# A decoder step on one core: x and the vectors taken from the host as features by tokens, the first gate and up run together, the first norm's sums spread out, and X's tiles moved in SBUF

## The chip, the cores and the metric

The kernel runs on one NeuronCore of one Trainium2 chip, as one program. The metric is the device time of one execution in microseconds (us). Engines are named as in the profile: PE is the matrix engine (PEld its weight loads), DVE the vector engine, ACT the scalar engine, POOL GpSimd, SP the engine that only issues DMAs here. A row "x5" counts instructions; DMAs are issued on the queue of the engine that is named.

## The reference

One inference step of a hybrid decoder layer, all in float32: 16 learned meta tokens and 256 prompt tokens, and 8 sequences of 4 sample tokens, together 304 tokens of width 2048.

```python
x = x + 0.5 * swiglu(rmsnorm(x, norm_ffn1), ffn1_w_gate, ffn1_w_up, ffn1_w_down)   # inner width 5632
z = rmsnorm(x, norm_mix) @ w_in                        # 6144 columns: u_pool, u_ssm, gates a and b
gates = sigmoid(z[..., 2048:] + b_gate)
a_out = pool_mix(u_pool, ...)                          # causal mean pooling, then 4 group matrices
s_out = gelu(s5_scan(u_ssm, ...)); s_out = s_out * sigmoid(s_out @ glu_w + glu_b)
merged = gate_a * (a_out @ w_branch_a) + gate_b * (s_out @ w_branch_b)
x = x + merged @ w_out
x = x + 0.5 * swiglu(rmsnorm(x, norm_ffn2), ffn2_w_gate, ffn2_w_up, ffn2_w_down)
y = rmsnorm(x, final_norm)
```

Here `swiglu(x, g, u, d) = (silu(x @ g) * (x @ u)) @ d`. Outputs are y for prompt and sample tokens and the new states of pooling and scan.

## The kernel before, in words

**Layout.** Activations lie with features on the 128 partitions and tokens along the free axis, 304 columns in the first feed-forward part and 288 (without meta tokens) later. A matmul has 128x128 of a weight as the stationary operand and 304 or 288 tokens moving.

**Precision.** Each float32 weight and activation is split into a high and a low part of a narrower format, and every product is three matmuls (`mm3`, L238 to L240): high times high, high weight times low activation, low weight times high activation. X holds the split norm input (without the factor 1/rms, which is applied to the result), H the split inner activations, Y the mixer's.

**Weights.** They are read once, in chunks of 4 x 128 rows by 256 columns (512 KB), in the order of one list. `Weights.load` issues a chunk's DMA on the SP queue (L132) into one of 3 buffers `raw`, `high` has ACT cast it to `whi` (L139), `low` has DVE take `wlo` = raw - whi (L148), `take` hands both to PE. `whi` and `wlo` have 4 buffers each. One chunk feeds 24 matmuls.

**Order.** Nothing is scheduled by a tool: each engine runs its instructions in the order in which the Python code emits them. After each chunk's matmuls `step` emits the next `high`, then what was posted (the work on a finished projection), the next `low`, the next `load`, and a few instructions of side work (the tables and scan of the S5 part, on DVE, ACT and POOL, paced by a rate per chunk).

**Stages.** ffn1 goes through 22 pairs of 128 inner columns: gate with 4 chunks, up with 4 chunks, 48 x 2 x 2 = 192 matmuls a pair; `gated` multiplies gate by 1/rms and applies silu, `upped` does up and the product, and `down` follows every second pair. Then come w_in, the pooling branch, the gates. In the mixer, `gated` stores its results z to DRAM on the SP queue, 8 times two tiles `msc` (L1079) for branch a, and 8 times two tiles `gsc` (L1087) for the gates of branch b, between the weight loads of that queue. The scan is side work on DVE at that time. Then come glu, branch b, w_out, ffn2, and the last norm.

**The opening.** x comes from the host as tokens by features. `load_x` fetches quarters of 512 features on SP (five DMAs each), turns them with PE's transposes (`tx`, L410), copies them to `x`, makes X, and has ACT square the tokens with a running sum (`sqt`, L417). `load_vectors` fetches the eight norm, bias and scale vectors on POOL and turns them on PE too (`vt`, L195). These are emitted between the chunks of pair 0's gate. The factor 1/rms is put on the diagonal of a matrix, and PE spreads it over the partitions (`rb`, L357); DVE copies it to `rs_y` (L362) and `gated` uses it (L455).

**PSUM.** Eight banks: four for projections (`pj`), three for smaller work, one long-lived.

Of the kernel before, what the change touches and what calls it, by code (L numbers as in the profile page):

```python
# [45 lines left out]
POOLRATE = 3.5  # L46
LATE = 8
LAG = 2
ROWS = 15
MAGIC = 12582912.0  # L50
RSQRT_BITS = 1597463007.0 - 2147483648.0
VROWS = {"norm_ffn1": (0, 16), "norm_mix": (16, 16), "norm_ffn2": (32, 16), "final_norm": (48, 16),
         "b_gate": (64, 32), "pool_scale": (96, 8), "ssm_d": (104, 8), "glu_b": (112, 8)}


# [24 lines left out]
def weight_order():  # L80

    def cols(name, c0, kd):
        return [(name, k0, KC, c0) for k0 in range(0, kd, KC)]

    def ffn_order(i):
        out = []
        down = lambda c: [(f"ffn{i}_w_down", c * FC, FC, q * 256) for q in range(8)]
        for p in range(NF // 2):
            out += cols(f"ffn{i}_w_gate", p * 256, KD) + cols(f"ffn{i}_w_up", p * 256, KD)
            if p >= 3 and p % 2 == 1:  # L90
                out += down((p - 3) // 2)
# [12 lines left out]
    for p in range(KW // 2):  # L104
        out += cols("glu_w", p * 256, KW)
    for p in range(KD // 2):
        out += cols("w_branch_b", p * 256, KW)
    for p in range(KD // 2):
        out += cols("w_out", p * 256, KD)
    return out + ffn_order(2)  # L110


class Weights:
# [8 lines left out]
    def load(self):  # L122
# [10 lines left out]
        self.loaded += 1  # L133

    def high(self):
        i = self.nhi
# [22 lines left out]
def setup(ctx, tc, I):  # L159
# [18 lines left out]
    nc.vector.memset(g.ones, 1.0)  # L178
    g.vec = g.const.tile([P, 120], F32, name="vec")
    g.hc = g.const.tile([P, NT + NTV + 2], F32, name="hc")  # L180
    return g


def load_vectors(g, pool):

    nc, I = g.nc, g.I
    vr = pool.tile([P, P], F32, name="vr")
    for name, (r0, n) in VROWS.items():
        src = I[name] if name == "final_norm" else I[name][0]
        nc.gpsimd.dma_start(vr[r0:r0 + n], src.rearrange("(k p) -> k p", p=P))  # L190
    nc.gpsimd.dma_start(g.hc, I["consts"])

    def turn(r0, n):
        ps = bank(g, "vt", aux=True)
        nc.tensor.transpose(ps[:, :n], vr[:n], g.ident[:n, :n])  # L195
        nc.vector.tensor_copy(g.vec[:, r0:n], ps[:, r0:n])

    return turn

# [42 lines left out]

def warm(g, func):

    t = g.act.tile([P, 1], F32, tag="warm", name=nm(g, "warm"))
    g.nc.scalar.activation(t, g.ones[:, :1], func)

# [33 lines left out]
class Norm:  # L281

    def __init__(self, g, gain, n, which):
        self.g, self.gain, self.n, self.which = g, gain, n, which
        self.x = []
        self.acc = None
        self.sqs = []
        self.ss = self.r = None  # L290
        self.toks = [(0, P), (P, P), (n - P, P)]
# [38 lines left out]
    def inverse(self):  # L330

        g, nc = self.g, self.g.nc
        y = g.act.tile([P, 3], F32, tag="rt", name=nm(g, "rt"))
        if self.ss is None:
            self.summed()
            ps = bank(g, "ss", aux=True)
            for i, (t0, tn) in enumerate(self.toks):
                nc.tensor.matmul(ps[:, 2 * i:2 * i + 2], self.acc[:, t0:t0 + tn], g.ones[:, :2], start=True, stop=True)
            rsqrt(g, y, ps[:, 0:6:2], [P, 3])
        else:  # L340
            nc.vector.tensor_reduce(y, self.ss, mybir.AxisListType.X, ALU.add)
            rsqrt(g, y, y, [P, 3])
        return y
# [8 lines left out]
    def spread(self):  # L352

        g = self.g
        pr = bank(g, "rb", aux=True)
        for i, (t0, tn) in enumerate(self.toks):
# [23 lines left out]

def load_x(g, tp, norm):

    nc, I = g.nc, g.I
    xp = I["x_prompt"][0]
    xs = I["x_sample"].rearrange("b s d -> (b s) d")
    Q = KC * P
    NQ = D // Q
    tks = []
    norm.ss = tp.tile([P, 3, NQ], F32, name="ss")
    nc.vector.memset(norm.ss, 1.0)  # L390
    rest = NT - 2 * P
    norm.toks = [(0, P), (P, P), (2 * P, rest)]

    def fetch(c):
        cs = slice(c * Q, (c + 1) * Q)
        tk = [tp.tile([P, Q], F32, tag=f"tok{i}", name=nm(g, "tok"), bufs=2) for i in range(3)]
        nc.sync.dma_start(tk[0][NMETA:], xp[0:P - NMETA, cs])
        nc.sync.dma_start(tk[0][:NMETA], I["meta_tokens"][:, cs])
        nc.sync.dma_start(tk[1], xp[P - NMETA:2 * P - NMETA, cs])
        nc.sync.dma_start(tk[2][:NMETA], xp[2 * P - NMETA:, cs])  # L400
        nc.sync.dma_start(tk[2][NMETA:rest], xs[:, cs])
        tks.append(tk)

    def turn(c):
        tk = tks[c]
        pss = []
        for f in range(KC):
            ps = bank(g, "tx", aux=f % 4 != 3)
            for t, (t0, tn) in zip(tk, norm.toks):
                nc.tensor.transpose(ps[:, t0:t0 + tn], t[:tn, f * P:(f + 1) * P], g.ident[:tn, :tn])  # L410
            pss.append(ps[:, :NT])
            norm.add([pss[f]], False)
            nc.vector.tensor_copy(g.x[c * KC + f], pss[f])
        for i, t in enumerate(tk):
            tn = P if i < 2 else rest
            sq = tp.tile([P, Q], F32, tag="sqt", name=nm(g, "sqt"), bufs=1)
            nc.scalar.activation(sq[:tn], t[:tn], AF.Square, accum_out=norm.ss[:tn, i, c:c + 1])  # L417

    return fetch, turn


def proj(g, name, c0, xs, n, kd, before=None):

    ps = [bank(g, "pj")[:, :n] for _ in range(2)]
    for k0 in range(0, kd, KC):
# [11 lines left out]

def ffn(g, pool, norm, i, hpart, done, before=None, last=False):

    nc, n = g.nc, norm.n  # L440
    h = []
    nchunk = NF // FC

    def gate_up(p):
        gs = []
        pg = proj(g, f"ffn{i}_w_gate", p * 256, norm.x, n, KD, before if p == 0 else None)
        if p == 0:
            g.post.append(norm.begin)

# [8 lines left out]

        g.post.append(gated if p else lambda: g.post.append(gated))
        pu = proj(g, f"ffn{i}_w_up", p * 256, norm.x, n, KD)  # L460

        def upped():
# [5 lines left out]
            h.extend(splits(g, us, n, hpart))  # L468

        g.post.append(upped)  # L470
        if p == 0 and before is not None:
            g.started()

# [726 lines left out]
def body(ctx, tc, I, O):  # L1200
    ctx.enter_context(tc.manual_schedule())
    g = setup(ctx, tc, I)
    nc = g.nc
    n1 = Norm(g, "norm_ffn1", NT, "X")
    n2 = Norm(g, "norm_mix", NT, "X")
    xsc = [g.dram.tile([P, NL], F32, name=f"xsc{m}") for m in range(KD)]
    with ExitStack() as c1:
# [3 lines left out]
        g.x = [xpool.tile([P, NT], F32, tag="x", name=f"x{m}", bufs=KD) for m in range(KD)]  # L1211
        ct = ExitStack()
        tp = ct.enter_context(tc.tile_pool(name="tok", bufs=1))
        warm(g, AF.Silu)
        fetch, turn = load_x(g, tp, n1)
        fetch(0)
# [9 lines left out]
        def before(c):  # L1226
            if c == 0:
# [7 lines left out]
            elif c + 1 < 4:  # L1235
                turn(c + 1)
            if c == 2:
                g.w.load()
            if c == 3:
                g.w.high()  # L1240
                g.w.low()
                g.w.load()
                vturn(16, 120)

        def started():
            ct.close()
            g.side, g.rate = ssm_setup(g), SETRATE
# [8 lines left out]
        g.started = started  # L1256
        ffn(g, fpool, n1, 1, "H", done, before)
        flush(g)
# [7 lines left out]
    with ExitStack() as c2:  # L1266
# [21 lines left out]

INS = ["x_prompt", "x_sample", "state_pool", "state_ssm_re", "state_ssm_im", "meta_tokens",
       "norm_ffn1", "ffn1_w_gate", "ffn1_w_up", "ffn1_w_down", "norm_mix", "w_in", "b_gate", "pool_w",  # L1290
       "pool_scale", "ssm_lambda_re", "ssm_lambda_im", "ssm_log_dt", "ssm_b_re", "ssm_b_im", "ssm_c_re",
       "ssm_c_im", "ssm_d", "glu_w", "glu_b", "w_branch_a", "w_branch_b", "w_out", "norm_ffn2",
       "ffn2_w_gate", "ffn2_w_up", "ffn2_w_down", "final_norm"]
OUTS = [(1, NPR, D), (NB, NS, D), (1, 1, HIST, WP), (1, NB, HIST, WP),
# [18 lines left out]
```

## Time and profile before

| what | value |
|---|---|
| time, median of 3 runs | 2366.49 us (2365.99 to 2367.37) |
| profiled execution | 2366.84 us, its span 2365.0 us |
| mean granted clock of PE | 0.998 |
| PE busy | 2344.9 us, 99% of the span, 17345 instructions |
| DVE busy | 1578.7 us, 67% |
| ACT busy | 980.1 us, 41% |
| POOL busy | 85.1 us, 4% |
| moved by DMA | 426.81 MB, 180 GB/s in the mean |

The profile is of one execution. Busy times of matmuls overlap, as they are pipelined, so how fast PE goes is read from the starts of successive matmuls. A row of the timeline gives start, duration, engine, line, operation, output and inputs with sizes, count, and in square brackets the idle time ahead of it with what ended it. A row of the waits reads: engine, line and output, what ended the wait, then total us, times, longest. In the groups stand busy time in us and mean ns of one, then the idle time before.

### The profile page before, as it was taken

Reading aid. Unit: us, or ns where it says so; the run is one execution under the profiler, and the core shown is the slowest. Engines: PE = TensorE matmul, PEld = TensorE weight load, DVE = VectorE, ACT = ScalarE, POOL = GpSimd, SP = SyncE. Lnnn points to the kernel's source line nnn. Section 1 sums busy time; section 2 is a strip of 40 time slices with the busy share of each in tenths; the row PEclk is TensorE's granted clock in tenths of the full one; section 3 lists DMA queues with packets and bytes.
Section 4 is the critical chain, followed back from the end, with each engine's and each line's share of the span. In section 5 each row is a group of like instructions: output and inputs, shape, how many; then the busy total and the mean of one; then the engine's idle time right before and its main releaser. Section 6 shows DMA issues by size and latency. Waiting matters only on the chain.

```text
span 2365.0 us, 42243 instructions
## 1 busy us (share of the span) xinstructions
PE 2344.9 (99%) x17345; PEld 2316.0 (98%) x17345; DVE 1578.7 (67%) x2405; ACT 980.1 (41%) x1443; POOL 85.1 (4%) x159
## 2 busy tenths in 40 slices
PE   8999999999999999999999999999999999999997
PEld 8999999999999999999999999999999999999997
DVE  6788777777545557689999775655555555555555
ACT  5333433333543335445454544433333333333334
POOL 1000000001000002000000040000000000000000
PEclk9999999999999999999999999999999999999999
DMA  6556566657555556657676585555555555555553
GB/s 190 160 155 189 188 205 208 203 189 190 182 175 161 153 159 195 202 167 221 230 226 205 187 265 182 159 170 168 163 169 164 167 166 165 169 163 167 166 164 112
DMA packets 386033, 426.81 MB, mean 180 GB/s; under 512 B 14604, under 2 KB 376304, under 8 KB 385832
## 3 DMA queue, kind: packets, MB, share of 16 engines
q1 hardware_dynamic: 375360, 375.57, 50.9%
q0 software_dynamic: 10480, 48.54, 6.4%
q8 instruction: 136, 2.23, 0.4%
q14 instruction: 57, 0.47, 0.1%
HBM read 396.04 MB, written 28.37 MB: 179 GB/s over the span
## 4 chain that ended last, share of the span: by engine, by line
PE 98%; DVE 1%; ACT 0%; DMA 0%; SPq 0%; issue 0%; ACTq 0%; DVEq 0%
PE pj L238 24%; PE pj L239 24%; PE pj L240 24%; PE dn L238 8%; PE dn L240 8%; PE dn L239 8%; PE bu L812 1%; PE yps L828 0%; PE tx L410 0%; PE bt L758 0%; DMA tok<-in_x_sample 0%; DVE wlo L148 0%; DVE acc L327 0%; ACT y L1183 0%; PE ty L1145 0%
## 5 line engine op out<-in xcount | busy, mean ns | idle before, releaser
L148 DVE TENSOR_TENSOR wlo<-raw,whi 128x1024 fp32r<-128x1024 f32 x698 | 853.1, 1224 | 598.8 <-ACT whi L139 597.7
L139 ACT CAST whi<-raw 128x1024 fp32r<-128x1024 f32 x698 | 732.8, 1051 | 1156.7 <-PE pj L239 684.8
L238 PE MATMUL pj<-X,whi 128*128 128x304 f32 (+1 forms) x2432 | 738.4, 304 | 0.1
L239 PE MATMUL pj<-X,whi 128*128 128x304 f32 (+1 forms) x2432 | 731.6, 301 | 0.0
L240 PE MATMUL pj<-X,wlo 128*128 128x304 f32 (+1 forms) x2432 | 730.6, 300 | 0.0
L238 PE MATMUL pj<-Y,whi 128*128 128x288 f32 x1728 | 509.8, 295 | 1.6 <-DVE Y L267 1.6
L239 PE MATMUL pj<-Y,whi 128*128 128x288 f32 x1728 | 510.2, 295 | 0.0
L240 PE MATMUL pj<-Y,wlo 128*128 128x288 f32 x1728 | 509.4, 295 | 0.0
L238 PEld LDWEIGHTS pj<-X,whi 128*128 128x128 f32 x2432 | 457.7, 188 | 11.1 <-issue 10.1
L239 PEld LDWEIGHTS pj<-X,whi 128*128 128x128 f32 x2432 | 459.2, 189 | 0.0
L240 PEld LDWEIGHTS pj<-X,wlo 128*128 128x128 f32 x2432 | 459.0, 189 | 0.0
L238 PEld LDWEIGHTS pj<-Y,whi 128*128 128x128 f32 x1728 | 325.2, 188 | 4.0 <-issue 2.1
L239 PEld LDWEIGHTS pj<-Y,whi 128*128 128x128 f32 x1728 | 325.0, 188 | 0.0
L240 PEld LDWEIGHTS pj<-Y,wlo 128*128 128x128 f32 x1728 | 324.6, 188 | 0.0
L238 PE MATMUL dn<-H,whi 128*128 128x304 f32 x704 | 213.3, 303 | 0.0
L240 PE MATMUL dn<-H,wlo 128*128 128x304 f32 x704 | 213.0, 303 | 0.0
L239 PE MATMUL dn<-H,whi 128*128 128x304 f32 x704 | 212.2, 301 | 0.0
L238 PE MATMUL dn<-X,whi 128*128 128x288 f32 x704 | 208.2, 296 | 0.0
L239 PE MATMUL dn<-X,whi 128*128 128x288 f32 x704 | 207.7, 295 | 0.0
L240 PE MATMUL dn<-X,wlo 128*128 128x288 f32 x704 | 207.5, 295 | 0.0
L238 PEld LDWEIGHTS dn<-X,whi 128*128 128x128 f32 x704 | 132.6, 188 | 0.0
L239 PEld LDWEIGHTS dn<-X,whi 128*128 128x128 f32 x704 | 132.4, 188 | 0.0
(261 smaller groups left out, 1835.5 us busy)
## 6 DMA issues: line engine op xcount, KB each, us to landing
raw<-in_ffn_w_gate SPq DMA_DIRECT2D x176, 512.0 KB, 3.6
raw<-in_ffn_w_up SPq DMA_DIRECT2D x176, 512.0 KB, 3.6
raw<-in_ffn_w_down SPq DMA_DIRECT2D x176, 512.0 KB, 3.5
raw<-in_w_in SPq DMA_DIRECT2D x96, 512.0 KB, 4.1
raw<-in_w_out SPq DMA_DIRECT2D x32, 512.0 KB, 4.4
esc<-ee POOLq DMA_DIRECT2D x16, 912.0 KB, 5.0
ee<-esc POOLq DMA_DIRECT2D x16, 912.0 KB, 7.1
raw<-in_w_branch_a SPq DMA_DIRECT2D x16, 512.0 KB, 4.4
```

Source lines behind the costliest of these rows:

```text
L139: self.g.nc.scalar.copy(hi, self.raw[i])
L148: self.g.nc.vector.tensor_tensor(lo, raw, hi.bitcast(F32), ALU.subtract)
L238: mm(ps, wh, x[0], start=start, stop=False)
L239: mm(ps, wh, x[1], start=False, stop=False)
L240: mm(ps, wl, x[0], start=False, stop=stop)
L812: g.nc.tensor.matmul(ps, self.mats[i][rows, 0, ri], self.u[i][rows], start=True, stop=True)
```

## The change

The host now gives x as 16 tiles of 128 features by 304 tokens (`xt`) and all vectors as one table of 128 x 120 (`vec`). `load_x` and `load_vectors` with their transposes and copies are gone, and so are the squares by tokens. A new function `opening` fetches the first four tiles of x on ACT's queue and the rest on SP's, lets PE multiply ones nine times (`stir`), splits the first chunks of gate and up quarter by quarter as their pieces come in, and runs gate and up of pair 0 chunk by chunk in turn, into four banks. The squares of x are made tile by tile, in the opening and in pair 1's gate, and summed by DVE; the sum over features on PE and the spreading of 1/rms then stand in pair 1, whose gate uses the banks for smaller work. What follows from pair 0's results (`held`) waits for that. The side work of ffn1 starts after pair 1's gate in place of pair 0's up. The tile `warm` of the first table load moves from the pool that holds X to that of constants and grows to 64 bytes; by the allocation X's tiles start at byte 66688 of a partition in place of 66656, and follow each other by 1216 bytes as before. H's and Y's tiles start at multiples of 64 bytes before and after.

```diff
-            out += cols(f"ffn{i}_w_gate", p * 256, KD) + cols(f"ffn{i}_w_up", p * 256, KD)
+            gate, up = cols(f"ffn{i}_w_gate", p * 256, KD), cols(f"ffn{i}_w_up", p * 256, KD)
+            out += [c for pair in zip(gate, up) for c in pair] if i == 1 and p == 0 else gate + up
...
+    def parted(self, i, k):
...
+        hi, lo = self.parts[i]
+        nc.scalar.copy(hi[:, k], self.raw[i][:, k])
+        nc.vector.tensor_tensor(lo[:, k], self.raw[i][:, k], hi[:, k].bitcast(F32), ALU.subtract)
...
+    nc.scalar.dma_start(g.vec, I["vec"])
...
-    t = g.act.tile([P, 1], F32, tag="warm", name=nm(g, "warm"))
-    g.nc.scalar.activation(t, g.ones[:, :1], func)
+    t = (pool or g.act).tile([P, 16 if pool else 1], F32, tag="warm", name=nm(g, "warm"))
+    g.nc.scalar.activation(t[:, :1], g.ones[:, :1], func)
...
+def opening(g, norm):
...
+    fetch(g.nc.scalar, 0, KC)
+    warm(g, AF.Silu, g.const)
+    for k in range(KC):
+        for i in range(2):
+            g.w.piece(i, k)
+    fetch(g.nc.sync, KC, 2 * KC)
+    g.w.load()
+    stir(g)
+    for k in range(KC):
+        norm.add(x[k:k + 1], False)
+        for i in range(2):
+            g.w.parted(i, k)
...
+    for c in range(KD // KC):
...
+        for u in range(2):
...
+            step(g)
+            if u == 0 and c + 2 < KD // KC:
+                fetch(g.nc.sync, (c + 2) * KC, (c + 3) * KC)
+            if c == 3:
+                if u == 0:
+                    g.w.high()
+                    g.w.low()
+                    g.w.load()
+                squares(1 + 2 * u)
+            elif c:
+                squares(1 + u)
...
+        if p == 1 and opened is not None:
+            def before(c):
+                if c < 2:
+                    opened[1](3)
+                if c == 1:
+                    g.post.append(norm.begin)
+
+            pg = gate(before, True)
+            held[0]()
+            g.post += [held[1], gated]
+            g.started()
...
-        g.w.load()
-        fetch(1)
-        vturn = load_vectors(g, tp)
-        vturn(0, 16)
-        turn(0)
-        g.w.high()
-        g.w.low()
-        g.w.load()
...
-                fetch(2)
-                g.w.load()
-                fetch(3)
-                g.w.load()
-                turn(1)
-                g.w.high()
-                g.w.low()
...
+        opened = opening(g, n1)
```

How the instructions stand now, at three places. Numbers behind names are those of the program's tiles. First the end of the transposes and the first matmuls on PE, before:

```order
L410 MATMUL tx_259<-ident,tok_141 128x128
L410 MATMUL tx_259<-ident,tok_142 128x128
L410 MATMUL tx_259<-ident,tok_143 128x48
L238 MATMUL pj_210<-X_166,whi_204 128x304
L239 MATMUL pj_210<-X_167,whi_204 128x304
L240 MATMUL pj_210<-X_166,wlo_206 128x304
```

and PE's first rows after:

```order
L392 MATMUL stir_148<-ones 128x128 x9
L249 MATMUL pj_194<-X_158,whi_162 128x304
L250 MATMUL pj_194<-X_159,whi_162 128x304
L251 MATMUL pj_194<-X_158,wlo_163 128x304
L249 MATMUL pj_195<-X_158,whi_162 128x304
L250 MATMUL pj_195<-X_159,whi_162 128x304
L251 MATMUL pj_195<-X_158,wlo_163 128x304
L249 MATMUL pj_196<-X_158,whi_166 128x304
```

The transposes are gone, and gate (pj_194, pj_195) and up (from pj_196 on) take turns. On ACT, the first rows before:

```order
L246 ACT_TABLE_LOAD
L246 ACTIVATE warm_127<-ones 128x1
L299 ACTIVATE X_166<-tx_162,vec 128x304
L299 ACTIVATE X_175<-tx_171,vec 128x304
L299 ACTIVATE X_184<-tx_180,vec 128x304
L299 ACTIVATE X_193<-tx_189,vec 128x304
```

and after:

```order
L206 DMA vec<-in_vec 128x120
L401 DMA x_110<-in_xt 128x304
L401 DMA x_111<-in_xt 128x304
L401 DMA x_112<-in_xt 128x304
L401 DMA x_113<-in_xt 128x304
L257 ACT_TABLE_LOAD
L257 ACTIVATE warm_130<-ones 128x1
L310 ACTIVATE X_158<-x_110,vec 128x304
L156 CAST whi_162<-raw_132 128x256
L156 CAST whi_166<-raw_134 128x256
L310 ACTIVATE X_170<-x_111,vec 128x304
```

Five DMAs now stand ahead of the table load, and the casts of the first chunks come in quarters behind each X. Second, the spreading of 1/rms on PE, which stood after the first chunk of pair 0's up, before:

```order
L240 MATMUL pj_494<-X_263,wlo_456 128x304
L357 MATMUL rb_572<-dg_539,ones 128x128 x2
L357 MATMUL rb_572<-dg_539,ones 128x48
L238 MATMUL pj_493<-X_312,whi_487 128x304
L239 MATMUL pj_493<-X_313,whi_487 128x304
```

and after:

```order
L251 MATMUL pj_529<-X_432,wlo_564 128x304
L364 MATMUL rb_693<-dg_626,ones 128x128 x3
L249 MATMUL pj_704<-X_158,whi_602 128x304
L250 MATMUL pj_704<-X_159,whi_602 128x304
L251 MATMUL pj_704<-X_158,wlo_628 128x304
```

It now stands between pair 1's gate (pj_529) and its up (pj_704). Third, the SP queue in the mixer, at the first of the 16 pairs of stores of z, before:

```order
L132 DMA raw_11652<-in_w_in 128x4x256
L132 DMA raw_11705<-in_w_in 128x4x256
L132 DMA raw_11748<-in_w_branch_a 128x4x256
L132 DMA raw_11785<-in_w_branch_a 128x4x256
L1079 DMA msc_10206<-z_11612 128x288
L1079 DMA msc_10207<-z_11615 128x288
L132 DMA raw_11832<-in_w_in 128x4x256
L132 DMA raw_11865<-in_w_in 128x4x256
```

and after:

```order
L135 DMA raw_11682<-in_w_in 128x4x256
L135 DMA raw_11719<-in_w_in 128x4x256
L1133 DMA msc_10140<-z_11546 128x288
L1133 DMA msc_10141<-z_11549 128x288
L135 DMA raw_11766<-in_w_branch_a 128x4x256
L135 DMA raw_11799<-in_w_branch_a 128x4x256
L135 DMA raw_11847<-in_w_in 128x4x256
L135 DMA raw_11893<-in_w_in 128x4x256
```

The two loads of w_branch_a that stood ahead of the two stores stand behind them, since the new opening emits two loads fewer ahead of the casts; so it is at each of the 16 pairs.

More of the change, by code (lines that the diff above doesn't have):

```diff
@@ L133, in load, with piece @@
         self.loaded += 1
+    def piece(self, i, k):
+        g = self.g
+        name, k0, kk, c0 = self.order[i]
+        if k == 0:
+            self.raw[i] = self.pool.tile([P, KC, 256], F32, tag="raw", name=nm(g, "raw"), bufs=RAW)
+            self.loaded += 1
+        g.nc.sync.dma_start(self.raw[i][:, k], g.I[name][0][(k0 + k) * P:(k0 + k + 1) * P, c0:c0 + 256])
+    def parted(self, i, k):
+        nc = self.g.nc
+        if k == 0:
+            self.parts[i] = tuple(self.pool.tile([P, KC, 256], F32R, tag=x, name=nm(self.g, x), bufs=AHEAD + 2)
+                                  for x in ("whi", "wlo"))
+            self.nhi += 1
+            self.nlo += 1
+        hi, lo = self.parts[i]
+        nc.scalar.copy(hi[:, k], self.raw[i][:, k])
+        nc.vector.tensor_tensor(lo[:, k], self.raw[i][:, k], hi[:, k].bitcast(F32), ALU.subtract)
+        if k == KC - 1:
+            self.raw.pop(i)
     def high(self):
@@ L178, in setup @@
     nc.vector.memset(g.ones, 1.0)
-    g.vec = g.const.tile([P, 120], F32, name="vec")
+    g.vec = g.const.tile([P, NVEC], F32, name="vec")
+    nc.scalar.dma_start(g.vec, I["vec"])
     g.hc = g.const.tile([P, NT + NTV + 2], F32, name="hc")
+    nc.gpsimd.dma_start(g.hc, I["consts"])
     return g
[L184 to L198, printed above, removed]
 def vcol(g, name, i):
@@ L333, in inverse @@
         y = g.act.tile([P, 3], F32, tag="rt", name=nm(g, "rt"))
[L334 to L342, printed above, removed]
+        self.summed()
+        ps = bank(g, "ss", aux=True)
+        for i, (t0, tn) in enumerate(self.toks):
+            nc.tensor.matmul(ps[:, 2 * i:2 * i + 2], self.acc[:, t0:t0 + tn], g.ones[:, :2], start=True, stop=True)
+        rsqrt(g, y, ps[:, 0:6:2], [P, 3])
         return y
@@ L354, in spread @@
         g = self.g
-        pr = bank(g, "rb", aux=True)
+        pr = bank(g, "rb", pool=g.pslong if self.long else g.psaux)
         for i, (t0, tn) in enumerate(self.toks):
@@ L378, in rsqrt @@
         cur = y
[L381 to L419, printed above, removed]
@@ L425, in proj @@
+def proj(g, name, c0, xs, n, kd, before=None, aux=False):
+    ps = [bank(g, "pj", aux=aux)[:, :n] for _ in range(2)]
     for k0 in range(0, kd, KC):
@@ L435, in proj, with ffn @@
     return ps
-def ffn(g, pool, norm, i, hpart, done, before=None, last=False):
+def ffn(g, pool, norm, i, hpart, done, opened=None, last=False):
     nc, n = g.nc, norm.n
@@ L442, in ffn @@
     nchunk = NF // FC
+    held = []
     def gate_up(p):
         gs = []
[L446 to L448 removed]
         def gated():
@@ L468, in upped @@
             h.extend(splits(g, us, n, hpart))
+        gate = lambda *a: proj(g, f"ffn{i}_w_gate", p * 256, norm.x, n, KD, *a)
+        if p == 0 and opened is not None:
+            pg, pu = opened[0]
+            held.extend((gated, upped))
+            return
+        if p == 1 and opened is not None:
[8 more added lines that the diff above has]
+            g.started()
+        else:
+            pg = gate()
+            if p == 0:
+                g.post.append(norm.begin)
+            g.post.append(gated if p else lambda: g.post.append(gated))
+        pu = proj(g, f"ffn{i}_w_up", p * 256, norm.x, n, KD)
         g.post.append(upped)
-        if p == 0 and before is not None:
-            g.started()
     def added(m, ps):
```

83 lines of the change are left out of this document (51 added, 32 removed).

## The prediction

> **What bounds the kernel now.** I read the page first, then the waits, then the timeline of the opening, then the mixer by windows and by its queue.
>
> ```profile
> span 2365.0 us, 42243 instructions
> PE 2344.9 (99%) x17345; PEld 2316.0 (98%) x17345; DVE 1578.7 (67%) x2405; ACT 980.1 (41%) x1443; POOL 85.1 (4%) x159
> ...
> PE vt L195 <- DMA vr<-in_norm_ffn: 5.4, 1, 5.4
> ...
> DVE wlo L148 <- ACT whi L139: 597.7, 473, 6.1
> ```
>
> PE fills 99% of the span. Its one long wait is 5.4 us at the start, and VectorE (DVE), which makes the low halves of the weights, has slack on average. So there are two ways to change the time: fewer or cheaper things on PE, or something that makes PE wait. The profiled execution took 2366.84 us (span 2365.0, 1.8 around it), 0.35 above the median of 2366.49; sums below are made against 2366.84 and then lowered by 0.35. A difference under 0.2%, 4.7 us, is what a measurement of this kernel cannot tell from none.
>
> The opening on PE (start, us busy, then the operation):
>
> ```profile
> 5.59 4.18 PE L410 MATMUL tx<-ident,tok 128*128 128x128 f32 x13
> ...
> 13.62 0.62 PE L238 MATMUL pj<-X,whi 128*128 128x304 f32 x1
> 14.04 0.46 PE L239 MATMUL pj<-X,whi 128*128 128x304 f32 x1
> ...
> 18.85 0.37 PE L240 MATMUL pj<-X,wlo 128*128 128x304 f32 x1
> 19.06 0.30 PE L238 MATMUL pj<-X,whi 128*128 128x304 f32 x1
> 19.48 2.24 PE L410 MATMUL tx<-ident,tok 128*128 128x128 f32 x12
> ...
> 34.20 0.30 PE L238 MATMUL pj<-X,whi 128*128 128x304 f32 x1
> ...
> 40.93 0.76 PE L357 MATMUL rb<-dg,ones 128*128 128x128 f32 x6
> 41.51 0.39 PE L238 MATMUL pj<-X,whi 128*128 128x304 f32 x1
> ```
>
> Transposes of x fill 5.6 to 13.6 us; weight matmuls then start one per 0.253 us (19 steps from 14.04 to 18.85) and from 19.06 one per 0.14 us (three steps in 0.42). From 18.85 to 34.20 the gate of pair 0 and the other transposes share PE; then comes its up. When pair 0 is over is told by the DVE instruction behind its last matmul, started 48.09 after a wait for PE, so PE ended it at about 48.0:
>
> ```profile
> 48.09 0.47 DVE L465 TENSOR_TENSOR us<-pj,rs_y 128x304 f32<-128x304 f32 x1 [0.73 <-PE pj L240]
> ```
>
> **Part 1, the opening.** Everything in those 48.0 us but the 192 matmuls of pair 0 goes (at 0.14 us they are 26.9). What comes in their place is bounded by these rows: windows (us; busy time of PE, PEld, DVE, ACT, POOL; clock, DMA share, GB/s), groups (busy us, mean ns) and one kind of load (KB each, us to landing).
>
> ```profile
> 0.00:10.00 10.00, 4.25 (x14) 2.23 (x14) 3.22 (x10) 3.78 (x7) 5.39 (x15) 1.00 0.78 215
> 20.00:25.00 5.00, 5.00 (x34) 4.34 (x34) 3.38 (x8) 4.72 (x11) 0.00 (x0) 1.00 0.81 261
> ...
> 0.74 1.28 ACT L246 ACT_TABLE_LOAD   x1 [0.74 <-PEq L1303]
> ...
> L299 ACT ACTIVATE X<-x,vec 128x304 fp32r<-128x304 f32 x16 | 7.9, 541 | 1.7 <-DVE x L476 1.5
> L322 ACT ACTIVATE sq<-x 128x304 f32<-128x304 f32 x15 | 6.4, 446 | 0.1
> ...
> raw<-in_ffn_w_gate SPq DMA_DIRECT2D x9, 512.0 KB, 4.8
> ...
> L148 DVE TENSOR_TENSOR wlo<-raw,whi 128x1024 fp32r<-128x1024 f32 x698 | 853.1, 1224 | 598.8 <-ACT whi L139 597.7
> L139 ACT CAST whi<-raw 128x1024 fp32r<-128x1024 f32 x698 | 732.8, 1051 | 1156.7 <-PE pj L239 684.8
> ```
>
> The first rows of x and the first pieces land at 3 to 5.4 us (4.8 for a whole 512 KB load, 5.4 for the first vector before). ACT has issued five DMAs and loaded its table (0.74 + 1.28, plus the issues) by then. Then X costs 0.54 and a cast of a quarter chunk between 0.26 (1.051/4) and 0.51 (if only elements beyond 304 are saved); I take 0.39 as the middle. First real matmul: about 6.2 us (5.7 to 6.9). ACT is the pace of the first chunk, 0.54 + 2 x 0.39 = 1.3 us per k against 12 matmuls x 0.14 = 1.7 (3.0 at half clock), so the first 48 matmuls end near 13 if the clock is half for 5 us, as in the rows above, or near 11 if the nine stirring matmuls bring it up. The next chunk decides more: ahead of it and with it go 8 x's of 0.156 MB, 8 pieces of 0.131, 0.061 of vectors and the chunk's 0.524: 2.88 MB. At the 261 GB/s of the second window that is 11.0 us, from about 1.0: 12.0; at the 215 of the first it is 14.4. Then 1.05 of ACT and 1.22 of DVE give the third matmul of chunk 2 at 14.3. Two matmuls stand before it, so the 6 x 24 = 144 matmuls left take 20.2 us from 14.0: pair 0 ends at 34.2 (32.6 with no wait at all; 36.7 at 215 GB/s).
>
> The sums of squares: 16 ACT squares of 0.446 = 7.1 us and 15 DVE adds, spread over 27 us of an ACT that is 41% busy in the mean and does one 1.05 us cast per 24 x 0.14 = 3.4 us; hidden, and if that cover were gone the end of pair 1's gate would be later by at most the part that delays a cast, 0.45 each. The x loads pass the SP queue ahead of chunks 4 and on: 8 x 0.156 MB, 4.8 us at 261 GB/s, while PE takes 3.4 us per 0.5 MB (156 GB/s asked); I count nothing for it beyond the bound just given. On PE, pair 1 now carries the sums, the broadcast (0.58, from 40.93 to 41.51) and a new wait: its up needs a bank that pair 0's gate frees only after DVE has copied the broadcast and read the bank. The sums at the kernel's end from the chain, and the two DVE steps:
>
> ```profile
> 2351.51 0.81 PE ss L338 x6
> ...
> 41.73 0.48 DVE L362 COPY rs_y<-rb 128x304 f32<-128x304 f32 x1 [2.80 <-PE rb L357]
> 42.24 0.86 DVE L455 TENSOR_TENSOR gs<-pj,rs_y 128x304 f32<-128x304 f32 x2
> ```
>
> The wait is 0.22 to DVE (41.51 to 41.73), 0.48 for the copy, half of 0.86 for the first bank's product and another 0.2 back to PE: 1.3 us. The sums are at most the 0.81 of the chain, where their last result is waited for; of two columns each they are nearer to nothing, and I take 0.3. With the broadcast 2.2. Behind these two DVE instructions in its queue stands the next low half, which PE needs 24 matmuls later: hidden. Gain of part 1: 48.0 - 34.2 - 2.2 = 11.6 (8 to 13.2).
>
> One loss is not in this sum. The rows above show steps of 0.253 us for 5.2 us behind the first ordinary matmul (13.62 to 18.85), though PE had turned x since 5.59. PE now has a gap of some 3 us ahead of chunk 2's third matmul; if that makes the slow steps come back for as long, 19 steps cost 19 x 0.113 = 2.1 us more. The Trainium skill, "TensorE: Matmul & The Clock Gate", says in Part 4 that transposes do not count as busy for the clock gate, with which those rows agree, and in Part 1 that about 3.4 us of idleness throttle the clock again, which no row here shows; by the latter rule a gap just under that would cost nothing.
>
> **Part 2, X aligned.** The small tile of the table load moves to another pool and takes 64 bytes there; every X tile starts 32 bytes further in SBUF, at a multiple of 64 bytes, as H's tiles did and do. Stretches of 384 matmuls that start as follows, with X before, H between, X after:
>
> ```profile
> 806.91 0.30 PE L238 MATMUL pj<-X,whi 128*128 128x304 f32 x1
> ...
> 860.78 0.30 PE L238 MATMUL dn<-H,whi 128*128 128x304 f32 x1
> ...
> 914.33 0.30 PE L238 MATMUL pj<-X,whi 128*128 128x304 f32 x1
> ```
>
> 53.87/384 = 140.3 ns with X (not aligned before), 53.55/384 = 139.5 with H (aligned). If the start is the reason, 0.84 ns x 4992 matmuls that read X at 304 columns = 4.2 us; if it is not, 0; if the 4416 that read X at 288 gain the same, 7.9. I take 4.2.
>
> **Part 3, what the order does to the mixer.** The opening emits fewer loads ahead: for the rest of the kernel the SP queue is one weight load ahead of the cast in place of three. While SP only loads, that is nothing: it goes on as buffers come free. But in the mixer it also stores z, 16 times in pairs, and two loads that stood ahead of each pair now stand behind it, where they wait for DVE's or ACT's z. SP, DVE and PE at the first pair, then landing times of weight loads (1060 to 1235, 1235 to 1330), two windows, and SP's waits:
>
> ```profile
> 1062.30 4.17 SPq L132 DMA_DIRECT2D raw<-in_w_branch_a  x2
> 1067.37 0.84 SPq L1079 DMA_DIRECT2D msc<-z  x2
> 1068.87 3.28 SPq L132 DMA_DIRECT2D raw<-in_w_in  x2
> ...
> 1070.51 1.23 DVE L148 TENSOR_TENSOR wlo<-raw,whi 128x1024 fp32r<-128x1024 f32 x1
> ...
> 1075.57 0.29 PE L238 MATMUL pj<-Y,whi 128*128 128x288 f32 x1
> ...
> DMA to landing us min/median/max: 3.4/4.5/7.7
> ...
> DMA to landing us min/median/max: 3.4/3.9/7.8
> ...
> 1060.00:1220.00 160.00, 159.94 (x1259) 148.51 (x1258) 150.46 (x220) 81.85 (x141) 6.92 (x13) 1.00 0.68 216
> 1220.00:1330.00 110.00, 110.00 (x867) 103.30 (x867) 96.28 (x134) 53.91 (x89) 2.13 (x4) 1.00 0.67 214
> ...
> SPq L1079 <- DVE z L1078: 21.3, 8, 3.7
> SPq L1087 <- ACT z L1025: 26.4, 8, 4.2
> ```
>
> The load issued at 1062.30, whose low half DVE makes at 1070.51 for PE's use at 1075.57, would be issued after the pair, at 1067.37 + 0.84 = 1068.2; with a landing of 4.2 (between the two medians) and the cast's 1.05 its low half starts at 1073.5, 3.0 us late. DVE runs in program order, so it stands still for that time, and everything behind it, the next z among it, comes later too: the loss repeats at the next pair and does not overlap with itself. 16 x 3.0 = 48 us of new idle time on DVE. Against it stand DVE's 270 - 246.7 = 23.3 us of idle time in the two windows, of which I let 14 be used up (60%; some of it waits on casts that come later as well), and its lead on PE, 1075.57 less 1071.74 = 3.8 us here, up to some 8 later; I take 5. PE loses 48 - 14 - 5 = 29. Bounds: landing of 3.4 (2.2 x 16 = 35, all idle time used, lead 5) gives 7; landing of 4.5, no idle time used and lead 5 gives 3.3 x 16 - 5 = 48.
>
> Everything else keeps its order: the side work that ssm_setup gives to DVE, ACT and POOL starts four chunks later, beside the same matmuls of ffn1.
>
> **Sum.** 2366.84 - 11.6 - 4.2 + 29 = 2380.0; against the median 2379.7.
>
> **Rivals.** First, the late loads stay hidden (this one ends on the other side): DVE's stall at each pair is used up before the next pair, because z's time is set by PE and not by DVE, or the load lands in 3.4 or less. It decides when the stall per pair is below (23.3 + 5)/16 = 1.8 us, against 3.0 worked out; for it speaks that DVE is only 91% busy (96.28/110) there, against it that z itself is a DVE instruction behind the stall. Time: 2366.5 - 15.8 = 2350.7, with up to 7 of loss 2358. Second, half hidden: a loss of 8 to 17 us gives 2359 to 2368, at or just under the time before. Third, the opening or X disappoints while the mixer loses as said: the slow steps' 2.1, a late second chunk's 2.5 and no gain of X, 4.2, would make 2379.7 + 8.8 = 2388.5. Against it: the 0.14 us steps from 19.06 on show no other stop than the transposes, and these go.
>
> **Chances.** The forecast (a loss of 18 to 45 in the mixer, 2369 to 2396 by itself) 0.55, with the third rival another 0.08; the first rival 0.21; the second 0.16. Below 2361.8 lie the first rival and a quarter of the second: faster 0.25. Between 2361.8 and 2371.2 lie the rest of the second and the low end of the forecast: same 0.15. Slower: 0.60. The range 2354 to 2394 leaves out half of the first rival and the upper end.
>
> **What would show it.** Right: weight matmuls from about 6 us; pair 0 over near 34 us; DVE's wait for casts, and the casts' for loads, growing in the mixer by some 45 us in all, and PE's wait for low halves there going from almost nothing to about 29 us, in steps of about 2 at each store pair; and 139.5 ns steps of X. Wrong: PE at 99% in the mixer's two windows with the store pairs 20 us apart as before; or a gap in PE within 10 to 20 us, well over 3 us.

## The result and the profile after

The changed kernel took 2401.39 us (median of 4 runs, 2400.7 to 2403.51) against 2366.91 before: slower, ratio 1.0146 with a 95% interval of 1.0134 to 1.0158. The forecast of 2379.7 had the direction, but the loss was 34.5 us where 13 were forecast, and the time lies above the range. The page of the changed kernel, whose profiled execution took 2400.7 us:

```profile
span 2398.9 us, 42169 instructions
PE 2352.2 (98%) x17319; PEld 2321.5 (97%) x17319; DVE 1578.9 (66%) x2406; ACT 977.8 (41%) x1441; POOL 81.1 (3%) x151
```

DVE does the same work as before (1578.9 against 1578.7 us), in a longer span. Where PE waited by the view of waits (total, times, longest):

```profile
PE bu L866 <- ACT row L871: 11.8, 5, 5.2
PE pj L249 <- DVE z L1078: 4.9, 3, 2.2
PE pj L249 <- ACT whi L165: 4.8, 4, 1.8
PE ss L348 <- DVE acc L338: 3.5, 2, 2.8
PE pj L251 <- DVE wlo L174: 2.9, 4, 0.7
```

The 5.4 us of waiting for vectors are gone, and many short waits for DVE and ACT are new. All of PE's waits together grew by 27.3 us (8.7 to 36.0), less than the loss; PE also goes more slowly behind some of them (below). So I counted the weight matmuls, of which both kernels have the same 16752 in nearly the same order, and compared when the one of the same number starts:

| place (number of the weight matmul) | before, us | after, us | difference |
|---|---|---|---|
| first one (0) | 13.6 | 6.0 | -7.7 |
| pair 1's gate begins (192) | 48.3 | 35.5 | -12.9 |
| pair 1's up begins (288) | 61.8 | 57.7 | -4.1 |
| mixer, ahead of the first pair of stores (7300) | 1061.5 | 1054.1 | -7.4 |
| mixer, near the eighth pair (8200) | 1197.8 | 1204.1 | +6.2 |
| behind the mixer's gates (9100) | 1330.2 | 1365.8 | +35.5 |
| last one (16751) | 2349.2 | 2383.9 | +34.6 |

So the opening gained 12.9 us, pair 1's gate gave 8.8 of them back, the steady part up to the mixer gained 3.3, and the mixer lost 42.9.

PE's timeline of the opening and of pair 1's gate:

```profile
5.97 0.40 PE L249 MATMUL pj<-X,whi 128*128 128x304 f32 x1 [1.10 <-ACT whi L156]
...
12.98 0.30 PE L251 MATMUL pj<-X,wlo 128*128 128x304 f32 x1
14.30 0.41 PE L249 MATMUL pj<-X,whi 128*128 128x304 f32 x1 [1.02 <-ACT whi L165]
...
15.56 0.41 PE L251 MATMUL pj<-X,wlo 128*128 128x304 f32 x1 [0.71 <-DVE wlo L174]
...
42.06 0.30 PE L251 MATMUL pj<-X,wlo 128*128 128x304 f32 x1
45.20 1.34 PE L348 MATMUL ss<-ones,acc 128*128 128x2 f32 x6 [2.83 <-DVE acc L338]
46.40 0.60 PE L249 MATMUL pj<-X,whi 128*128 128x304 f32 x1
...
52.11 0.30 PE L250 MATMUL pj<-X,whi 128*128 128x304 f32 x1
...
57.74 0.38 PE L249 MATMUL pj<-X,whi 128*128 128x304 f32 x1 [1.17 <-DVE gs L492]
```

The first weight matmul is at 5.97 and the third of chunk 2 at 15.56. In pair 1's gate no matmul starts between 42.06 and 45.20 (2.83 us of it idle), because DVE has not added the squares; the sums then take 1.2 us, and 23 matmuls follow in 5.71 us (46.40 to 52.11), 0.248 each in place of 0.14. The granted clock shows it, 0.76 in this window (columns as before; the clock is the third from the end):

```profile
40.00:50.00 10.00, 7.17 (x37) 6.95 (x37) 6.52 (x20) 4.41 (x7) 0.00 (x0) 0.76 0.22 69
```

Why the adds are late is to be read on ACT and DVE: ACT's wait for `sq` up to 50 us in all, a window, and the rows ahead of the sums, ACT's first:

```profile
ACT sq L333 <- DVE acc L338: 6.6, 4, 1.7
...
30.00:45.00 15.00, 12.36 (x89) 12.11 (x87) 11.17 (x18) 9.44 (x16) 0.00 (x0) 1.00 0.56 170
...
40.13 1.03 ACT L165 CAST whi<-raw 128x1024 fp32r<-128x1024 f32 x1
42.90 1.48 ACT L333 ACTIVATE sq<-x 128x304 f32<-128x304 f32 x3 [1.74 <-DVE acc L338]
...
41.20 1.23 DVE L174 TENSOR_TENSOR wlo<-raw,whi 128x1024 fp32r<-128x1024 f32 x1 [1.46 <-ACT whi L165]
42.34 2.71 DVE L338 TENSOR_TENSOR acc<-acc,sq 128x304 f32<-128x304 f32 x5
```

The kernel gives `sq` two buffers. The next square on ACT (42.90) must wait until DVE has added one (42.34 on); in DVE's order that add stands behind a low half (41.20), which waits for ACT's cast (40.13). So ACT and DVE wait for each other by turns, though in this stretch ACT is busy for only 9.44 of 15 us and DVE for 11.17.

The mixer, first the windows of before and after over the same matmuls (about number 7290 to 9100), then what DVE's low halves waited for in them, before and after:

```profile
1060.00:1330.00 270.00, 269.94 (x2124) 251.81 (x2123) 246.73 (x353) 135.76 (x229) 9.04 (x17) 1.00 0.67 215
...
DVE wlo L148 <- ACT whi L139: 14.3, 16, 2.0
```

```profile
1052.00:1366.00 314.00, 288.57 (x2132) 264.49 (x2131) 246.74 (x354) 135.49 (x228) 9.04 (x17) 0.96 0.56 182
...
DVE wlo L174 <- ACT whi L165: 60.1, 24, 5.8
...
DMA to landing us min/median/max: 3.4/4.8/9.2
```

DVE is busy for 246.7 us in both; it is idle for 23.3 of 270 before and for 67.3 of 314 after. That is 44.0 us more, and the low halves' waits for casts alone grew by 45.8 (14.3 to 60.1). PE itself waited 25.4 us in the mixer, where it had waited for nothing before; the other 17.5 of the 42.9 are slower steps, and the granted clock fell from 1.00 to 0.96. Loads landed 4.8 us after their issue in the median (the line below the waits: shortest, median, longest); before it was 4.5 and 3.9 in the two parts of the mixer. One pair of stores, the first, in the timelines of SP, ACT, DVE and PE:

```profile
1060.00 0.82 SPq L1133 DMA_DIRECT2D msc<-z  x2
1060.91 1.54 SPq L135 DMA_DIRECT2D raw<-in_w_branch_a  x2
...
1065.62 1.04 ACT L165 CAST whi<-raw 128x1024 fp32r<-128x1024 f32 x1 [7.10 <-DMA raw<-in_w_branch_a]
1066.57 1.35 ACT L871 COPY row<-bu 128x304 f32<-128x304 f32 x4
...
1066.70 1.23 DVE L174 TENSOR_TENSOR wlo<-raw,whi 128x1024 fp32r<-128x1024 f32 x1 [3.48 <-ACT whi L165]
...
1067.03 1.46 PE L866 MATMUL bu<-u,bc 32*128 32x304 f32 x6 [2.85 <-ACT row L871]
```

Read it from the DVE row upwards: DVE stood for 3.48 us, until ACT had cast; ACT had stood for 7.10 until the load landed, 4.7 us after its issue; and the load was issued right behind the stores, which had waited for z. PE's row shows a second way: the copies `row` stand on ACT behind the same late cast, and PE waited 2.85 us for them.

### The profile page after: what moved, and what is told of

It reads as the page before. It is cut to its first block, busy times and chain, and to the rows that moved or that the text cites. A ratio compares the mean times of both kernels' runs of the same rounds, so it can differ in the third digit from the quotient of the medians.

```text
span 2398.9 us, 42169 instructions
## 1 busy us (share of the span) xinstructions
PE 2352.2 (98%) x17319; PEld 2321.5 (97%) x17319; DVE 1578.9 (66%) x2406; ACT 977.8 (41%) x1441; POOL 81.1 (3%) x151
## 4 chain that ended last, share of the span: by engine, by line
PE 86%; DVE 7%; DMA 3%; ACT 2%; issue 1%; SPq 0%; ACTq 0%; DVEq 0%
PE pj L249 20%; PE pj L250 20%; PE pj L251 20%; PE dn L251 8%; PE dn L250 8%; PE dn L249 8%; DVE wlo L174 2%; DMA raw<-in_w_in 2%; DMA raw<-in_w_branch_a 1%; ACT whi L165 1%; DVE row L903 1%; DVE row L926 1%; PE bu L866 0%; DVE acc L338 0%; DVE row L938 0%
## 5 line engine op out<-in xcount | busy, mean ns | idle before, releaser
L250 PEld LDWEIGHTS dn<-H,whi 128*128 128x128 f32 x704 | 132.4, 188 | 0.0
L250 PEld LDWEIGHTS dn<-X,whi 128*128 128x128 f32 x704 | 132.4, 188 | 0.0
```

Of the source, the lines that this page charges most:

```text
L250: mm(ps, wh, x[1], start=False, stop=False)
```

## The experiments

Theory A: the loss is the order on SP, two weight loads newly behind each pair of stores. Rival B: the side work, the banks or X's place. All ratios are to the kernel before, with 95% intervals.

**Three loads ahead again.** The changed kernel with

```diff
         opened = opening(g, n1)
+        g.w.load()
+        g.w.load()
```

> The changed kernel with two more weight loads emitted right behind the opening, so that SP is again three loads ahead of the casts and no load stands newly behind a store of z; nothing else differs. Theory A (the loads behind the 16 store pairs make DVE stand still and PE wait): the 42.9 us that the mixer lost come back, 2401.4 - 43 = about 2358.5, and DVE's idle time in the mixer falls from 67 to about 23 us. Rival B (the mixer lost time because the side work or the banks fell otherwise, or because of X's place): still 2395 to 2401.

It took 2356.71 us, ratio 0.9959 (0.9947 to 0.9972): faster than before, by 10.3 us. In the mixer's window DVE's low halves waited as before the change:

```profile
1050.00:1321.00 271.00, 270.40 (x2137) 252.27 (x2136) 248.49 (x356) 136.61 (x230) 9.07 (x17) 1.00 0.67 216
...
DVE wlo L174 <- ACT whi L165: 13.4, 17, 1.9
```

Between matmuls 7300 and 9100 it gained 0.7 on the kernel before, so the whole 42.9 came back with two lines. Rival B falls.

**The order alone, in the kernel before.**

```diff
     g.w.low()
-    g.w.load()
+    g.steps = getattr(g, 'steps', 0) + 1
+    if g.steps not in (40, 41):
+        g.w.load()
```

> The kernel before with two of its weight loads left to later steps (the 40th and 41st step issue none), so that from ffn1 on SP is one load ahead in place of three; x, opening, norm and X stay as before. Theory A: 2366.9 + 43 = about 2410, all of the loss in the mixer. Rival B: 2367, no change.

It took 2413.95 us, ratio 1.0203 (1.0188 to 1.0219); 47 us lost.

```profile
1062.00:1375.00 313.00, 289.54 (x2121) 266.64 (x2121) 245.61 (x351) 134.78 (x227) 9.04 (x17) 0.95 0.56 181
...
DVE wlo L148 <- ACT whi L139: 59.2, 23, 6.2
```

The waits are those of the changed kernel (59.2 against 60.1), without any of the rest of the change. By the count of matmuls the loss is 0.2 us up to number 6700, 1.7 at 7300 and 45.0 at 9100, and stays there.

**Two loads ahead.** The changed kernel with

```diff
         opened = opening(g, n1)
+        g.w.load()
```

> The changed kernel with one more load behind the opening: SP is two loads ahead, and one load in place of two stands newly behind each pair of stores. Theory A (what counts is when the first delayed load's low half is due on DVE): that is now the second chunk behind the store, 3.2 to 4.2 us later in DVE's order, so the stall of 3.6 us nearly goes and 2357 to 2363 is left. Rival (each load behind a store costs its half): 2401.4 - 22 = 2379.

It took 2364.08 us, ratio 0.9988 (0.9979 to 0.9997). From matmul 7300 to 9100 it lost 5.6 us, an eighth of the 42.9, where one of the two loads is still behind each pair. A load behind a store does not cost by itself. The result fits that it costs when its cast and low half are due sooner than store, landing and cast take (6.7 us in the rows above), and those of the second load are due later.

**Half of the stores elsewhere.** The changed kernel, one load ahead, with

```diff
-                        nc.sync.dma_start(gsc[2 * p + f], gate(pg[f], KD + 2 * p + f))
+                        nc.scalar.dma_start(gsc[2 * p + f], gate(pg[f], KD + 2 * p + f))
```

> The changed kernel (one load ahead) with the 16 stores gsc issued on ACT's queue; the 16 stores msc stay on SP. So 8 of the 16 pairs no longer hold up weight loads. Theory A (each pair on SP stops DVE for about 3.6 us): of the 42.9 us lost in the mixer the part behind the first eight pairs stays, 13 to 17, and the rest comes back: 2401.4 - 26 to 30 = 2371 to 2375. Rival (being one load ahead is itself the loss, stores or not): 2401.

It took 2380.9 us, ratio 1.006 (1.0046 to 1.0073). The difference to the kernel before went from -8.7 us at matmul 7300 to +15.7 at 8500, about where the stores go over to gsc, and was +16.0 at 9100: the loss stops there. So it is the stores on SP that make one load ahead too few. The msc half cost 24.4 us, more than the 13 to 17 that were expected; in the changed kernel it was 24.0 up to the same number (-7.4 to +16.6) and 18.9 from there on. The expectation split the loss at matmul 8200, too early. DVE's waits up to 1240 us and from there on:

```profile
DVE wlo L174 <- ACT whi L165: 27.2, 13, 5.6
...
DVE wlo L174 <- ACT whi L165: 9.6, 8, 2.7
```

**X's place alone, in the kernel before.**

```diff
-        warm(g, AF.Silu)
+        warm(g, AF.Silu, g.const)
```

with `warm` as in the change.

> The kernel before with the tile of the first table load in the pool of constants, 64 bytes, so that X's tiles start at a multiple of 64 bytes; nothing else differs. Theory A (X read from the better start costs PE 0.66 to 0.84 ns less per matmul at 304 columns): 2366.9 - 3.3 to 4.2 in ffn1 and the first projections, some 0 to 1 later, 2362 to 2363.5. Rival: the steps of 140.3 ns came from what else runs beside them, 2366.9.

It took 2361.93 us, ratio 0.9979 (0.997 to 0.9988): 5.0 us faster (2.8 to 7.1). The stretch of 384 matmuls that read X, whose steps were 140.3 ns, starts and ends in this kernel at

```profile
804.75 0.30 PE L238 MATMUL pj<-X,whi 128*128 128x304 f32 x1
...
858.42 0.30 PE L238 MATMUL dn<-H,whi 128*128 128x304 f32 x1
```

53.67/384 = 139.8 ns, where the H stretch had 139.5. The gain grows with the matmuls that read X: 0.7 us at number 384, 3.0 at 7104, where those of 304 columns end, and 5.4 at the last one in the profiled execution. So 2.4 of it came where X is read at 288 columns.

**The sum over features later.** On top of three loads ahead:

```diff
-                if c == 1:
+                if c == 2:
                     g.post.append(norm.begin)
```

> As the kernel with three loads ahead, and the sum over features on PE stands after pair 1's third gate chunk, not its second, so that DVE has added the squares by then. Theory A (PE stood still for 3.1 us there, and the slow steps of 0.253 us that followed came from that standstill): the wait, about 24 x 0.113 = 2.7 us of slow steps and some 0.6 of slow sums go, 6.4 in all: 2352. Rival C (the slow steps would come anyway, only the wait goes): 2355.5. Rival D (the broadcast now waits for DVE in place of the sum, since its chain of 3 us starts later): 2357 to 2359.

It took 2354.52 us, ratio 0.9949 (0.9937 to 0.9962); its five runs (2353.1 to 2355.5) lie below all five with three loads ahead alone (2356.0 to 2358.5), but the gain is 2.2 and not 4.5. PE in this kernel:

```profile
48.15 0.80 PE L348 MATMUL ss<-ones,acc 128*128 128x2 f32 x6 [1.10 <-DVE acc L338]
...
55.10 0.38 PE L249 MATMUL pj<-X,whi 128*128 128x304 f32 x1 [2.03 <-DVE gs L492]
...
55.87 0.46 PE L251 MATMUL pj<-X,wlo 128*128 128x304 f32 x1
```

The sum still waits 1.1 us, the wait of up grew to 2.03, and slow steps came behind that one (13, until 59.2). Part of the time only moved.

**PE kept busy through the wait.** On top of three loads ahead, 13 multiplications of ones ahead of the sum:

```diff
-                    g.post.append(norm.begin)
+                    g.post += [lambda: stir(g, 13), norm.begin]
```

> As the kernel with three loads ahead, and 13 more multiplications of ones stand on PE ahead of the sum over features, where PE waited 2.8 us for DVE: PE is busy in that time but the sum is no earlier. Theory A (the slow steps of 0.253 us behind the wait come from PE's idleness): steps stay at 0.14 us, 13 x 0.113 and faster sums: 2356.7 - 1.5 to 2.5. Rival (they come from the small matmuls of sum or broadcast): slow steps stay, 2356.7 or more.

It took 2354.67 us, ratio 0.9952 (0.994 to 0.9965), 2.0 us under three loads ahead alone, though measured with another set and with runs (2354.5 to 2359.3) that overlap with that kernel's, so the time alone shows no gain. First that kernel's PE, then this one's:

```profile
45.73 0.80 PE L348 MATMUL ss<-ones,acc 128*128 128x2 f32 x6 [2.46 <-DVE acc L338]
...
47.03 0.45 PE L250 MATMUL pj<-X,whi 128*128 128x304 f32 x1
47.29 0.46 PE L251 MATMUL pj<-X,wlo 128*128 128x304 f32 x1
```

```profile
42.62 3.06 PE L392 MATMUL stir<-ones 128*128 128x128 f32 x26
45.74 0.83 PE L348 MATMUL ss<-ones,acc 128*128 128x2 f32 x6
46.43 0.38 PE L249 MATMUL pj<-X,whi 128*128 128x304 f32 x1
46.66 0.30 PE L250 MATMUL pj<-X,whi 128*128 128x304 f32 x1
```

The sum comes at the same time, but with useless work in the gap the slow steps do not come: 42.62 to 45.74 is as long as the standstill in the changed kernel (42.06 to 45.20). So, by one profiled execution each, PE's idleness brings them, not the small matmuls. The Trainium skill, "TensorE: Matmul & The Clock Gate", Part 1, gives about 3.4 us of idleness for that; here waits of 2.46 us (the row of 45.73) and, in the changed kernel, 2.83 were enough.

**Two ways to be rid of both waits.** First, 13 squares in the opening, and the broadcast one chunk earlier:

```diff
-                squares(1 + u)
+                squares(2 + (u if c == 1 else 0))
...
-                if c < 2:
+                if c == 0:
                     opened[1](3)
...
+                if c == 3:
+                    held[0]()
...
             pg = gate(before, True)
-            held[0]()
```

> As the kernel with three loads ahead; 13 of the 16 squares in the opening in place of 10, the other 3 ahead of pair 1's first gate chunk, so that DVE has the sums ready; and the broadcast of 1/rms after pair 1's third gate chunk in place of its fourth, so that pair 0's banks are free when up begins. Expected: the waits of 3.1 and 1.2 us and the slow steps behind them go: 2356.7 - 5 to 6 = about 2351. Rival (the squares now hold up the casts and lows of the opening by as much, 3 x 0.45 us of ACT and 3 x 0.55 of DVE): 2354 to 2357.

It took 2356.29 us, 0.995 (0.9937 to 0.9964): no gain on three loads ahead. PE waited longer for the sums, not shorter:

```profile
48.67 0.58 PE L348 MATMUL ss<-ones,acc 128*128 128x2 f32 x4 [3.45 <-DVE acc L338]
```

Second, all 16 squares in the opening, each group ahead of its step's cast:

```diff
+            if c:
+                squares(3 if u else 2 + (c == 2))
             step(g)
...
-                squares(1 + 2 * u)
-            elif c:
-                squares(1 + u)
...
-                if c < 2:
-                    opened[1](3)
-                if c == 1:
+                if c == 0:
                     g.post.append(norm.begin)
+                if c == 2:
+                    held[0]()
```

> As the kernel with three loads ahead; all 16 squares in the opening, each group on ACT ahead of the cast of its step and not behind it; the sum over features after pair 1's first gate chunk, the broadcast after its second. Theory A (the squares came late because ACT stood at a cast that waits for a buffer which PE frees): PE waits for the sum under 0.5 us, no slow steps, no wait of up: 2356.7 - 5 = about 2351.5. Rival (squares ahead of casts make PE wait for casts): 2354 to 2357.

It took 2357.67 us, 0.9961 (0.9948 to 0.9973). The sum was waited for all the same, and matmuls of the opening now waited for low halves:

```profile
31.20 0.41 PE L251 MATMUL pj<-X,wlo 128*128 128x304 f32 x1 [0.71 <-DVE wlo L174]
...
45.20 1.41 PE L348 MATMUL ss<-ones,acc 128*128 128x2 f32 x6 [2.42 <-DVE acc L338]
```

Both accounts of why the squares are late fell. The traces show the two buffers of `sq` again: up to 50 us, ACT waited for DVE's adds 5 times, 8.2 us, in each of these two kernels, against 4 times and 6.6 with three loads ahead alone. No run gave `sq` more buffers, so what they would bring is not shown.

**The broadcast earlier, with PE kept busy.** On top of the multiplications:

```diff
+                if c == 3:
+                    held[0]()
 
             pg = gate(before, True)
-            held[0]()
```

> As the kernel with the multiplications of ones ahead of the sum, and the broadcast after pair 1's third gate chunk. Theory A (up waits 1.2 to 1.4 us for DVE to read pair 0's bank): that wait goes, 2354.7 - 1.3 = 2353.4. Rival (PE waits for DVE's chain at the broadcast instead): 2354.7 or more.

It took 2354.44 us, 0.9944 (0.9931 to 0.9958), within the spread of the one without (2354.67). The wait of up is gone from the list of waits; in the profiled execution the opening had slow steps instead. It is the fastest of the lot, 12.7 us under before, but no better than two others within what the runs tell.

**No multiplications at the start.** On top of three loads ahead:

```diff
-STIR = 9
+STIR = 0
```

> As the kernel with three loads ahead, without the nine multiplications of ones ahead of the first weight matmul. Theory A (PE's slow steps end only after some us of work): weight matmuls from about 6 us go at 0.253 for about 5 us, 19 x 0.113 = 2.1 us later at the first chunks' end, of which 1 to 1.5 are hidden behind the wait for chunk 2: 2357 to 2358.5. Rival: no difference in the steps, 2356.7.

It took 2357.51 us, 0.9959 (0.9946 to 0.9973), the same as with them. Slow steps stood in it from 7.06 to 10.35, as expected. But they stood in four of the nine profiled kernels that have the nine multiplications as well (until 9.4 to 10.6 us; matmul 24 came at 11.1 to 11.6, against 9.7 to 9.9 in three others). In the last two matmul 24 came at 10.7 and 11.0, because PE waited for a cast. One execution each does not show whether the multiplications help.

## Why the prediction was right or wrong

**Opening: right.** The first weight matmul was put at 6.2 and came at 5.97; the third of chunk 2 at 14.3 and came at 15.56; the end of pair 0 was to come 13.8 us earlier and came 12.9 earlier. The waits in chunk 2 (1.02 and 0.71 us) were shorter than the 3 us feared.

**Pair 1: the term of 2.2 us was mis-sized; it was 8.8.** I costed the sums at 0.3, the broadcast and the wait behind it at 1.9, and the squares and adds at nothing, hidden in an ACT that is 41% busy in the mean. The last two came at 2.0 (55.74 to 57.74). But the sums waited for DVE's adds, 3.1 us from start to start, took 1.2 themselves, and 23 slow steps followed, 2.6 us. The step that failed is "hidden": it was argued from busy shares, and the squares and adds were late because they waited for each other through two buffers (ACT 6.6 us, four times), in a stretch where ACT was busy for 63% and DVE for 74%. The slow steps were named in the prediction, at the wrong gap.

**X: the total was right, partly by luck.** 4.2 us were forecast, all of them at 304 columns (0.84 ns a matmul) and none at 288. In the changed kernel 3.3 came up to the mixer and about 0.9 behind it; alone it gave 5.0 (2.8 to 7.1), of which, by the count, 3.0 came at 304 columns and 2.4 at 288: the one was put too high, the other at nothing.

**Mixer: the mechanism was right as far as DVE, the size was 42.9 and not 29.** Three numbers made the size. The stall at a pair was put at 3.0 us, with a landing of 4.2. The landing's median became 4.8, and the 16 waits of the low half behind a pair, read one by one in the trace, are 1.5 to 5.8 us long, 3.6 each. The first 15, 54.0 us, lie in the window, in place of 48: 6.0 us too little. (Behind the 16th, at 1370 us, the difference grows no more: 35.5 at matmul 9100 and at 9250.) The idle time that could be used up was put at 14; it was 54.0 - 44.0 = 10.0. DVE's lead over PE was to save 5 us; PE lost 42.9 of DVE's 44.0, so it saved 1.1.

The last link, from DVE to PE, was wrong. PE was to wait some 29 us for low halves; in the mixer it waited 2.2 us for them. Its 25.4 us of waits were 11.4 for the copies `row` of ACT ahead of `bu`, 4.9 for z, 3.8 for casts, 3.1 ahead of `yps` and those 2.2, and slower steps made up the rest. The prediction followed the stall through DVE alone; but ACT stood at the late load first (7.10 us at the first pair), and what PE needed from ACT stood behind it. A lead on low halves does not help there. That much the trace shows; how much of the loss goes this way, and whether the slower steps cost anything by themselves, no run tested.

**The rivals.** "Hidden" was given 0.21 and "half hidden" 0.16; both fell with the loss of 42.9: z does stand behind the stall, as DVE's instruction for `msc` and as ACT's for `gsc`. Of the third, the disappointing opening, a form came true beside the forecast. The range failed because it let the mixer's upper bound of 48 and a poor opening hardly stand together: 2366.8 - 4.1 - 4.2 + 42.9 = 2401.4 is the sum with the sizes as measured. The mixer's error alone (13.9 us) would have given 2393.6 and the opening's alone (11.6 less 4.1, 7.5 us) 2387.2, both within the range.

## What to carry to other kernels

A queue runs in the order of its program: before code is moved, look at what each load stands behind, not only at how many are under way. Two loads fewer ahead cost nothing in most of this kernel and 43 us at 16 pairs of stores that wait for a result. Where a stall repeats on an engine that is over 90% busy in its stretch, expect most of it as a loss of the whole (here 42.9 of 54.0 us), size it by the landing under its own conditions, and follow it through every engine that stands behind the late load, here ACT as well as DVE. And do not cost new side work by a busy share, be it that of the stretch: follow what each of its instructions waits for, a free buffer included.

## What the runs showed of the hardware that was not expected

- Waits of 2.46 and 2.83 us on PE, each with the six short sums behind it, were followed by 13 and 23 matmuls at 0.25 us, and one of 2.03 us (before 55.10, with the sum later) by 13. With PE at work on ones through the same time there were none. The length alone does not decide: in the mixer of the changed kernel steps of 0.24 us came behind a wait of 1.87 us (the one that ended at 1293.4), and steps of 0.13 behind one of 2.24 (at 1104.0).
- Nine multiplications of ones ahead of the first weight matmul did not reliably bring full speed: with the same start, the first chunk's matmuls went at 0.14 us in five kernels' profiles and at 0.25 for 3 to 4 us in four. The clock column shows 1.00 from 5.9 to 11 us in all nine, so there only the starts of the matmuls tell.
- X's tiles 32 bytes further on, at a multiple of 64 bytes, are worth 0.5 to 0.7 ns a matmul of 304 columns: 140.3 to 139.8 ns in the kernel before and 139.5 in the changed one; alone 5.0 us of the time (2.8 to 7.1). Only these two places were tried, so that the multiple of 64 is what counts is not shown.
